# Fixing TensorE's instruction order in a two-layer encoder, and putting weight splits behind the layer norms

## The chip, the cores and the metric

The kernel runs on one core of one Trainium2 chip. The metric is the device time of one execution in microseconds, less is better. The engines named below are TensorE (PE, the matrix products), VectorE (DVE), ScalarE (ACT), GpSimd (POOL) and SyncE (SP, which issues the DMA transfers of the weights).

## The reference

256 tokens of width 1024 and 256 memory tokens go through two layers in float32. Each layer has three residual parts, each followed by a layer norm:

```python
x = layer_norm(x, emb_ln_g, emb_ln_b)
for l in range(2):
    h = hybrid_mixer(x, ...)                     # one product with w_in, then three branches
    x = layer_norm(alpha * x + h, ln_g[l, 0], ln_b[l, 0])
    h = memory_cross_attention(x, mem, ...)      # 4 heads of 256 over the memory's keys and values
    x = layer_norm(alpha * x + h, ln_g[l, 1], ln_b[l, 1])
    h = conv_ffn(x, ...)                         # (silu(conv(gate)) * up) @ w_out, inner width 2816
    x = layer_norm(alpha * x + h, ln_g[l, 2], ln_b[l, 2])
```

The mixer's branches are a differential attention (4 heads, two softmaxes each, rotary positions), a neighbourhood attention (8 heads, a bias for each pair of positions) and a gated short convolution; their results are weighted by gates, summed and multiplied by `w_mix_out`.

## The kernel before

**Products.** Every product is made three times, of operands split into a high and a low part (`mm3`, L243 to L247): high by high (L245), and the two mixed ones (L246, L247). A split (`split_from`, L249 to L251) is two instructions: ACT copies the source, rounded, to the high part (L250), and DVE subtracts that from the source to get the low part (L251). Weights are split so on the chip, and so is every activation that a product reads.

**Weights.** They come as 356 units of 128 x 1024 float32 (512 KB), each used once. `prefetch` (L1090) issues a unit's DMA on SP's queue into one of 4 raw buffers (L1094) and splits it into one of 8 pairs of high and low buffers. It runs 7 units (`LOOK`) ahead of the step that reads the unit. A unit is 24 products of 256 columns, or as many columns in wider products. The first units are the four of the memory's values (`v`) and then those of its keys (`k`); `start` (L480) calls `prefetch(4)` and then `inputs(6)` (L1108), which issues the token tiles, units up to the sixth, and the gain and offset of the first norm (`ln_consts`, DMAs on L1102).

**The order of the work.** The program is a list of steps, made before anything is issued by a planner (`interleave`, L114). Each `Step` has a function, a cost in TensorE time, a latency after which its successor may start, the units it reads and the PSUM banks it takes and gives back. A main sequence is interleaved with side sequences that are spawned (norms, the heads of an attention) and with fills (the products for the memory's keys and values). A unit counts 2.62, the scores of the differential attention have a latency of 5.5, those of the other two attentions 4.0, transposes 1.4 or 1.8. `emit` (L1144) then walks the list, prefetches and calls each step's function.

The list is the program's order. It isn't yet the order in which an engine executes: a scheduler of the compiler orders each engine's instructions by when it reckons them ready, and by priority, which follows the program's order. Only SP is held to the program's order (`manual_schedule`, L1155). PE, ACT and DVE are ordered by the scheduler.

**Places of the list that matter below** (the functions' names; a unit between them in brackets):

- start: the embedding's two norms, then four units of memory values, two units of memory keys, the first transposes of the normed tokens
- layer 1 and alike layer 2, differential attention (`rope` L546 with `swap` L548 and `turn` L554; `diff_group` L568, its score products on L531 and L532): ... `turn`, [vb 3], [gc 0], scores, scores, [gc 1], [gc 2], transposes, transposes, ...
- neighbourhood attention (`near_pair`, L674): [g2 0], scores, scores, [g2 1], [g2 2], transposes, transposes, scores, ...
- cross-attention (`cross_head`, L823): ..., transposes of head 3, scores of head 4, values of head 3, transposes of head 4, values of head 4, a wait for all heads, then the units of the output product (`tok_out`, L872)
- the norm ahead of layer 2's feed-forward: the last products of `tok_out` for token tile 1, two groups of transposes of token tile 0 with the warm-up product (`keep_warm`, L999) between, then the units `fm` of `up_first` (L1005), then `ffn_in` (L1013) and `ffn_out` (L1051)

**The norms.** The residual sum and its statistics (`ln_part`, L345: sum L350, statistics L355) run on DVE as each group of columns is finished. `ln` (L360) then gives a norm step for each of two token tiles (aggregate L368, square root on ACT L369, subtract and scale by the gain L373, reciprocal L385, scale by the deviation and add the offset L378), and transposes on PE (L414), whose results are split (L250, L251) to be the next products' operand. `residual` (L985) spawns the norms of token tiles 0 and 1 after their last products. In the kernel before, `urgent` (L253) records by engine the last norm operation (the sums, statistics, root, scale, and the split of a turned tile), and `behind` (L258) makes the split of each unit prefetched later wait in its engine's order behind the one recorded. The wait is one of order alone. The warm-up product is 8 products of the identity matrix, written to a bank that nothing reads.

Of the kernel before, what the change touches and what calls it, by code (L numbers as in the profile page):

```python
# [21 lines left out]
AF = mybir.ActivationFunctionType  # L22
ALU = mybir.AluOpType
AX = mybir.AxisListType

P = 128
# [168 lines left out]
def rd(t):  # L195
    return t.bitcast(F32)


class Encoder:
    LOOK = 7  # L200
    ACC, ATT = 3, 5
    TB = 10
    BIG = 22
# [45 lines left out]
    def split_from(self, src, ah, al):  # L249
        return (self.nc.scalar.copy(ah, src),  # L250
                self.nc.vector.tensor_tensor(out=al, in0=src, in1=rd(ah), op=ALU.subtract))  # L251

    def urgent(self, ins):  # L253

        self.ahead[ins.ins.engine] = ins.ins.name
        return ins

    def behind(self, ins):  # L258
        name = self.ahead.get(ins.ins.engine)
        if name is not None:  # L260
            self.tc.add_manual_dep(ins.ins, name, NOSYNC, reason="behind a layer norm")

    def proj_f8(self, u, xa, o):

# [71 lines left out]
        return self.tok(n, l, 0, xn, evac, tiles)  # L336


    def ln_consts(self, g, b):
        nc = self.nc  # L340
        self.lng, self.lnb = self.big(), self.big()
        self.load(self.lng, g.partition_broadcast(P))
        self.load(self.lnb, b.partition_broadcast(P))

    def ln_part(self, i, c, acc=None):  # L345

        nc, x = self.nc, self.x[i]
        sl = slice(*c)
        if acc is not None:
            self.urgent(nc.vector.scalar_tensor_tensor(out=x[:, sl], in0=x[:, sl], scalar=ALPHA, in1=acc,  # L350
                                                       op0=ALU.mult, op1=ALU.add))
        if c[0] == 0:
            self.T["st", i] = self.small(24).rearrange("p (c s) -> p c s", c=4)
        for q in range(c[0] // 256, c[1] // 256):
            self.urgent(nc.vector.bn_stats(self.T["st", i][:, q], x[:, 256 * q:256 * q + 256]))  # L355
        if i == 0 and c[0] == 0:

            nc.scalar.activation(self.small(1), self.T["st", 0][:, 0, 0:1], AF.Sqrt, bias=self.epsb, scale=0.0)

    def ln(self, i, nxt, rel, pre=2.6):  # L360

        st = {}
        w = 512 if i == 0 else 256

        def norm():
            nc, x = self.nc, self.x[i]
            mv, rs = self.small(2), self.small(1)
            nc.vector.bn_aggr(mv, self.T["st", i])  # L368
            self.urgent(nc.scalar.activation(rs, mv[:, 1:2], AF.Sqrt, bias=self.epsb, scale=1.0))  # L369

            def sub(h):
                sl = slice(w * h, w * h + w)
                return nc.vector.scalar_tensor_tensor(out=x[:, sl], in0=x[:, sl], scalar=mv[:, 0:1],  # L373
                                                      in1=self.lng[:, sl], op0=ALU.subtract, op1=ALU.mult)

            def scale(h):
                sl = slice(w * h, w * h + w)
                return nc.vector.scalar_tensor_tensor(out=x[:, sl], in0=x[:, sl], scalar=rs,  # L378
                                                      in1=self.lnb[:, sl], op0=ALU.mult, op1=ALU.add)

            if nxt is not None:
                for h in range(D // w):
                    sub(h)
                    if h == 0:
                        nc.vector.reciprocal(rs, rs)  # L385
                    self.urgent(scale(h))
                return

            n, nb = D // w, self.small(1)
            sub(0)  # L390
            nc.vector.reciprocal(rs, rs)
            r = nc.vector.scalar_tensor_tensor(out=nb, in0=mv[:, 0:1], scalar=-1.0, in1=rs,
                                               op0=ALU.mult, op1=ALU.mult)
            sl = slice(w * (n - 1), D)
            nc.scalar.activation(x[:, sl], x[:, sl], AF.Identity, bias=nb, scale=rs)
            nc.gpsimd.tensor_tensor(out=x[:, sl], in0=x[:, sl], in1=self.lng[:, sl], op=ALU.mult)
            nc.gpsimd.tensor_tensor(out=x[:, sl], in0=x[:, sl], in1=self.lnb[:, sl], op=ALU.add)
            for h in range(n - 1):
                if h:
                    self.tc.add_manual_dep(sub(h).ins, r.ins.name, NOSYNC, reason="order of the last rows")  # L400
                scale(h)
            for h in range(n):
                sl = slice(w * h, w * h + w)
                eng = nc.scalar if h % 2 else nc.sync
                eng.dma_start(self.out[i * P:(i + 1) * P, sl], x[:, sl])

        def transp(h):
            nc, n = self.nc, w // P
            if i == 0 and h == 0:
                self.T[nxt] = self.act_tile()  # L410
            a = self.T[nxt]
            pt = self.att()[:, :w].rearrange("p (k t) -> p k t", k=n)
            for k in range(n):
                nc.tensor.transpose(pt[:, k], self.x[i][:, (n * h + k) * P:(n * h + k + 1) * P], self.ident)  # L414
            t, k = n * h // 4, n * h % 4
            for ins in self.split_from(pt, a.his[t][:, k:k + n, i * P:(i + 1) * P],
                                       a.los[t][:, k:k + n, i * P:(i + 1) * P]):
                self.urgent(ins)

        yield Step(norm, 0, pre, rel=rel)  # L420
        if nxt is not None:
            for h in range(D // w):
                yield Step(lambda h=h: transp(h), 0.11 * w / P, 0.3 if h < D // w - 1 else 1.0, acq=1, rel=1)
# [56 lines left out]
    def start(self):  # L480

        nc = self.nc
        self.epsb = self.cst.tile([P, 1], F32, tag="epsb", name="epsb")
        nc.vector.memset(self.epsb, EPS)
        nc.scalar.activation(self.small(1), self.epsb, AF.Sqrt, bias=self.epsb, scale=1.0)
        hi = self.wp.tile([P, 1024], F32R, tag="hi", name=self.nm("hi"), bufs=self.WB)
        lo = self.wp.tile([P, 1024], F32R, tag="lo", name=self.nm("lo"), bufs=self.WB)

        def unit(j, m):
            if j:  # L490
                self.prefetch(j + 1)
                return
            raw, sl = self.t512(), slice(2 * m, 2 * m + 512)
            nc.sync.dma_start(raw, self.aps["w"][0][:, sl])
            self.split_from(raw, hi[:, sl], lo[:, sl])
            if m:
                self.split.append((hi, lo))
        self.load_mem(unit)
        self.prefetch(4)
        self.inputs(6)  # L500
# [406 lines left out]
    def main(self):  # L907
# [7 lines left out]
        for l in range(DEPTH):  # L915
# [55 lines left out]

            um = l == DEPTH - 1
            if um:
                yield Step(self.keep_warm, acq=1, rel=1)
                yield from self.up_first(l, xn, [f"a{l}0", f"a{l}1"])
            yield Wait(f"a{l}0", f"a{l}1")
            yield from self.ffn_in(l, xn, 4 if um else 0)
# [7 lines left out]
    def residual(self, steps, name, xn):  # L985
# [13 lines left out]
    def keep_warm(self):  # L999

        o = self.att()
        for _ in range(8):
            self.nc.tensor.matmul(o[:, :P], self.ident, self.ident, start=True, stop=True)  # L1003

    def up_first(self, l, xn, waits):  # L1005

# [83 lines left out]
    def prefetch(self, upto):  # L1090
        nc = self.nc
        while len(self.split) < min(upto, len(self.order)):
            raw = self.raw()
            nc.sync.dma_start(raw, self.aps["w"][len(self.split)])  # L1094
            hi = self.wp.tile([P, 1024], F32R, tag="hi", name=self.nm("hi"), bufs=self.WB)
            lo = self.wp.tile([P, 1024], F32R, tag="lo", name=self.nm("lo"), bufs=self.WB)
            for ins in self.split_from(raw, hi, lo):
                self.behind(ins)
            self.split.append((hi, lo))

    def load(self, t, src):
# [42 lines left out]
    def emit(ctx, self, tc, aps, out):  # L1144
        nc, PS = tc.nc, bass.MemoryType.PSUM
        self.nc, self.tc, self.aps, self.out = nc, tc, aps, out
        self.uid, self.split, self.bias, self.ahead = 0, [], {}, {}
# [4 lines left out]
        self.sm = ctx.enter_context(tc.tile_pool(name="sm", bufs=4))  # L1152
        self.psa = ctx.enter_context(tc.tile_pool(name="psa", bufs=self.ACC, space=PS))
        self.psb = ctx.enter_context(tc.tile_pool(name="psb", bufs=self.ATT, space=PS))
        with tc.manual_schedule(engines={mybir.EngineType.SP}):  # L1155
            pos = 0
            for s in self.steps:
                if s.units:
                    pos += len(s.units)
                    self.prefetch(pos + self.LOOK)  # L1160
                s.fn(*self.split[pos - len(s.units):pos])


def _layout(a, order):
# [56 lines left out]
```

## Time and profile before

| | before |
|---|---|
| median of 3 executions | 1135.65 us (1134.47 to 1135.90) |
| profiled execution | 1135.06 us |
| its span | 1133.3 us |
| mean granted TensorE clock | 0.994 |
| DMA moved in the span | 208.53 MB, mean 184 GB/s |

The span is the time from the first to the last instruction in the trace; the profiled execution's own time is 1.8 us longer. The clock is the share of full speed that the chip grants TensorE. Rows of the timeline give the start, the duration of all instructions of the row together (overlaps counted once), engine, line, operation, output <- inputs, and the number of instructions; in brackets stands the engine's idle time before the row and what ended it. Products are pipelined: a duration of 0.28 us for one doesn't mean that the next starts 0.28 us later. The 356 units are most of the DMA traffic, and a unit's transfer lands a median of 4.0 us after its issue.

### The profile page before, as it was taken

The page shows a single profiled execution, that of the slowest core. Times are in us where ns is not written, and L with a number is a line of the kernel's source. Part 1 is how long each engine was busy: PE and PEld are TensorE (multiplying, and loading weights), DVE is VectorE, ACT ScalarE, POOL GpSimd, SP SyncE. Part 2 cuts the span into 40 slices and gives each one's busy share as a digit, 9 for nine tenths or more (in the row PEclk, how much of TensorE's full clock was granted, in tenths as well). Part 3 has the DMA queues.
Part 4 walks back from the last instruction along what each step waited for, and adds up shares of the span by engine and source line. Part 5 has one row for each costly group of instructions (what it writes and reads, how often), then busy time and mean ns, then how long its engine had stood idle before and what let it go on. Part 6 is the DMA issues. An engine that isn't in the chain of part 4 may idle for free.

```text
span 1133.3 us, 18595 instructions
## 1 busy us (share of the span) xinstructions
PE 1103.8 (97%) x7340; PEld 1014.8 (90%) x7340; DVE 798.9 (70%) x1198; ACT 612.7 (54%) x958; POOL 12.4 (1%) x18
## 2 busy tenths in 40 slices
PE   7999999999999999999999999999999979999997
PEld 6899998888898999998889999888889879999986
DVE  6788888666864876665586888865787576666644
ACT  5556767445453565554445667744536436555540
POOL 0000000000000000000000000000000000000001
PEclk9999999999999999999999999999999989999999
DMA  8785437567563666565747544556746444665551
GB/s 297 245 262 170 136 135 232 183 189 241 168 186 99 200 204 186 182 181 189 263 143 231 174 148 167 179 185 197 256 145 201 140 149 150 186 185 180 182 180 37
DMA packets 60471, 208.53 MB, mean 184 GB/s; under 512 B 7008, under 2 KB 8288, under 8 KB 60384
## 3 DMA queue, kind: packets, MB, share of 16 engines
q1 hardware_dynamic: 59952, 206.83, 56.9%
q8 instruction: 57, 0.93, 0.3%
q10 hardware_dynamic: 432, 0.52, 0.1%
q14 instruction: 30, 0.25, 0.1%
HBM read 204.18 MB, written 1.05 MB: 181 GB/s over the span
## 4 chain that ended last, share of the span: by engine, by line
PE 66%; DVE 3%; ACT 1%; DMA 1%; issue 1%; DVEq 0%; ACTq 0%; SPq 0%
PE acc L245 18%; PE acc L246 18%; PE acc L247 18%; PE att L246 3%; PE att L247 3%; PE att L245 3%; DMA raw<-in_w_dram 1%; DVE lo L251 1%; PE att L414 0%; ACT hi L250 0%; DVE s L355 0%; DVE big L251 0%; PE att L617 0%; PE att L851 0%; PE att L1003 0%
## 5 line engine op out<-in xcount | busy, mean ns | idle before, releaser
L251 DVE TENSOR_TENSOR lo<-raw,hi 128x1024 fp32r<-128x1024 f32 x355 | 431.8, 1222 | 237.1 <-ACT hi L250 235.6
L250 ACT CAST hi<-raw 128x1024 fp32r<-128x1024 f32 x355 | 370.7, 1050 | 333.1 <-PE acc L246 155.5
L245 PE MATMUL acc<-big,hi 128*128 128x256 f32 x1376 | 391.0, 285 | 3.1 <-ACT big L294 1.2
L246 PE MATMUL acc<-big,hi 128*128 128x256 f32 x1376 | 390.2, 284 | 1.9 <-DVE big L251 1.9
L247 PE MATMUL acc<-big,lo 128*128 128x256 f32 x1376 | 390.2, 284 | 0.6 <-DVE lo L251 0.6
L245 PEld LDWEIGHTS acc<-big,hi 128*128 128x128 f32 x1376 | 263.3, 192 | 5.1 <-ACT big L294 1.8
L246 PEld LDWEIGHTS acc<-big,hi 128*128 128x128 f32 x1376 | 263.6, 192 | 3.0 <-DVE big L251 2.6
L247 PEld LDWEIGHTS acc<-big,lo 128*128 128x128 f32 x1376 | 263.6, 192 | 1.2 <-DVE lo L251 1.1
L245 PE MATMUL acc<-hi,big 128*128 128x512 f32 x584 | 230.1, 396 | 6.1 <-ACT hi L250 6.0
L246 PE MATMUL acc<-lo,big 128*128 128x512 f32 x584 | 230.8, 395 | 0.5 <-DVE lo L251 0.5
L247 PE MATMUL acc<-hi,big 128*128 128x512 f32 x584 | 228.0, 393 | 0.0
L245 PEld LDWEIGHTS acc<-hi,big 128*128 128x128 f32 x584 | 110.5, 190 | 27.1 <-ACT hi L250 6.5
L247 PEld LDWEIGHTS acc<-hi,big 128*128 128x128 f32 x584 | 110.7, 190 | 23.0
L246 PEld LDWEIGHTS acc<-lo,big 128*128 128x128 f32 x584 | 110.9, 190 | 21.2 <-DVE lo L251 1.2
L246 PE MATMUL att<-lo,big 128*128 128x256 f32 (+1 forms) x228 | 72.6, 319 | 0.0
L245 PE MATMUL att<-hi,big 128*128 128x256 f32 (+1 forms) x228 | 72.4, 318 | 0.0
L247 PE MATMUL att<-hi,big 128*128 128x256 f32 (+1 forms) x228 | 72.3, 318 | 0.0
L250 ACT CAST big<-att 128x512 fp32r<-128x512 f32 (+2 forms) x64 | 28.1, 458 | 45.8 <-PE att L247 25.8
L251 DVE TENSOR_TENSOR big<-att,big 128x512 fp32r<-128x512 f32 (+2 forms) x64 | 32.1, 518 | 27.7 <-ACT big L250 27.2
L245 PEld LDWEIGHTS att<-hi,big 128*128 128x128 f32 x228 | 43.3, 190 | 4.9
L246 PEld LDWEIGHTS att<-lo,big 128*128 128x128 f32 x228 | 43.3, 190 | 4.5
L247 PEld LDWEIGHTS att<-hi,big 128*128 128x128 f32 x228 | 43.3, 190 | 3.1
(145 smaller groups left out, 948.2 us busy)
## 6 DMA issues: line engine op xcount, KB each, us to landing
raw<-in_w_dram SPq DMA_DIRECT2D x355, 512.0 KB, 4.0
t<-in_bias_dram SPq DMA_DIRECT2D x16, 256.0 KB, 5.5
big<-in_ln_g_dram SPq DMA_DIRECT2D x6, 512.0 KB, 5.5
big<-in_ln_b_dram SPq DMA_DIRECT2D x6, 512.0 KB, 6.2
raw<-in_memT_dram SPq DMA_DIRECT2D x6, 512.0 KB, 4.4
big<-big SPq DMA_DIRECT2D x16, 128.0 KB, 2.3
x<-in_x_dram SPq DMA_DIRECT2D x4, 256.0 KB, 7.9
t<-in_memT_dram SPq DMA_DIRECT2D x3, 256.0 KB, 7.9
```

Of the source, the lines that this page charges most:

```text
L245: mm(o, lh, rh, start=first, stop=False)
L246: mm(o, lh, rl, start=False, stop=False)
L247: mm(o, ll, rh, start=False, stop=last)
L250: return (self.nc.scalar.copy(ah, src), self.nc.vector.tensor_tensor(out=al, in0=src, in1=rd(ah), op=ALU.subtract))
L251: self.nc.vector.tensor_tensor(out=al, in0=src, in1=rd(ah), op=ALU.subtract))
```

## The change

TensorE is held to the program's order, as SP is. The instructions of a norm (sums and statistics, the norm step, the transposes and splits of the turned tile) are traced with a priority as if they stood 2000 instructions earlier. A list `parts` keeps the two split instructions of every unit. `hold` records the last four norm operations of an engine (the root on ACT, the last scale on DVE, the splits of a turned tile on both) and puts the splits of all units from position `pos + 4` on behind them, those already traced too; `behind` does the same for units prefetched later. The sums and statistics are recorded no more. The warm-up step and its function are removed.

```diff
 class Encoder:
     LOOK = 7
+    NEAR = 4
...
-    def urgent(self, ins):
-
-        self.ahead[ins.ins.engine] = ins.ins.name
-        return ins
-
-    def behind(self, ins):
-        name = self.ahead.get(ins.ins.engine)
-        if name is not None:
-            self.tc.add_manual_dep(ins.ins, name, NOSYNC, reason="behind a layer norm")
...
+    def ahead(self):
+
+        return self.tc.high_priority(offset=2000)
+
+    def hold(self, ins):
+
+        names = self.last.setdefault(ins.ins.engine, [])
+        names.append(ins.ins.name)
+        del names[:-4]
+        for parts in self.parts[self.pos + self.NEAR:]:
+            self.behind(parts)
+
+    def behind(self, parts):
+        for p in parts:
+            for name in self.last.get(p.ins.engine, ()):
+                self.tc.add_manual_dep(p.ins, name, NOSYNC, reason="behind a layer norm")
+
...
     def ln_part(self, i, c, acc=None):
 
+        with self.ahead():
+            self.ln_sum(i, c, acc)
+
+    def ln_sum(self, i, c, acc):
...
         def norm():
+            with self.ahead():
+                normalise()
+
+        def normalise():
...
-                    self.urgent(scale(h))
+                    done = scale(h)
+                self.hold(root)
+                self.hold(done)
                 return
...
         def transp(h):
+            with self.ahead():
+                turn(h)
+
+        def turn(h):
...
-                self.urgent(ins)
+                self.hold(ins)
...
             if um:
-                yield Step(self.keep_warm, acq=1, rel=1)
                 yield from self.up_first(l, xn, [f"a{l}0", f"a{l}1"])
...
-            for ins in self.split_from(raw, hi, lo):
-                self.behind(ins)
+            self.parts.append(self.split_from(raw, hi, lo))
+            self.behind(self.parts[-1])
             self.split.append((hi, lo))
...
-        with tc.manual_schedule(engines={mybir.EngineType.SP}):
-            pos = 0
+        with tc.manual_schedule(engines={mybir.EngineType.SP, mybir.EngineType.PE}):
             for s in self.steps:
                 if s.units:
-                    pos += len(s.units)
-                    self.prefetch(pos + self.LOOK)
-                s.fn(*self.split[pos - len(s.units):pos])
+                    self.pos += len(s.units)
+                    self.prefetch(self.pos + self.LOOK)
+                s.fn(*self.split[self.pos - len(s.units):self.pos])
```

More of the change, by code (lines that the diff above doesn't have):

```diff
@@ L349, in ln_part @@
         if acc is not None:
-            self.urgent(nc.vector.scalar_tensor_tensor(out=x[:, sl], in0=x[:, sl], scalar=ALPHA, in1=acc,
-                                                       op0=ALU.mult, op1=ALU.add))
+            nc.vector.scalar_tensor_tensor(out=x[:, sl], in0=x[:, sl], scalar=ALPHA, in1=acc,
+                                           op0=ALU.mult, op1=ALU.add)
         if c[0] == 0:
@@ L354, in ln_part @@
         for q in range(c[0] // 256, c[1] // 256):
-            self.urgent(nc.vector.bn_stats(self.T["st", i][:, q], x[:, 256 * q:256 * q + 256]))
+            nc.vector.bn_stats(self.T["st", i][:, q], x[:, 256 * q:256 * q + 256])
         if i == 0 and c[0] == 0:
@@ L368, in norm @@
             nc.vector.bn_aggr(mv, self.T["st", i])
-            self.urgent(nc.scalar.activation(rs, mv[:, 1:2], AF.Sqrt, bias=self.epsb, scale=1.0))
+            root = nc.scalar.activation(rs, mv[:, 1:2], AF.Sqrt, bias=self.epsb, scale=1.0)
             def sub(h):
@@ L494, in unit @@
             nc.sync.dma_start(raw, self.aps["w"][0][:, sl])
-            self.split_from(raw, hi[:, sl], lo[:, sl])
+            parts = self.split_from(raw, hi[:, sl], lo[:, sl])
             if m:
+                self.parts.append(parts)
                 self.split.append((hi, lo))
@@ L997, in residual @@
         yield Spawn(f"{name}1", self.ln(1, xn, 2 if name[0] != "f" else 3, 3.4))
[L999 to L1003, printed above, removed]
     def up_first(self, l, xn, waits):
@@ L1146, in emit @@
         self.nc, self.tc, self.aps, self.out = nc, tc, aps, out
-        self.uid, self.split, self.bias, self.ahead = 0, [], {}, {}
+        self.uid, self.split, self.bias = 0, [], {}
+        self.pos, self.parts, self.last = 0, [], {}
         self.cst = ctx.enter_context(tc.tile_pool(name="cst", bufs=1))
```

## Prediction

> **What bounds the kernel now.** I read the page's head first: if TensorE (PE) is the bound, only the microseconds in which it stands or runs slowly can be won or lost.
>
> ```profile
> span 1133.3 us, 18595 instructions
> PE 1103.8 (97%) x7340; PEld 1014.8 (90%) x7340; DVE 798.9 (70%) x1198; ACT 612.7 (54%) x958; POOL 12.4 (1%) x18
> ```
>
> PE is busy 1103.8 of 1133.3 us, VectorE (DVE) 70%, ScalarE (ACT) 54%. So 29.5 us is all that better ordering could ever save, while every wait put into PE's stream adds its full length. The view of busy time by stretches gives PE's pace in an undisturbed stage and its speed in a disturbed one (columns: length, then PE, weight loads, DVE, ACT and POOL busy, granted clock, DMA share, GB/s).
>
> ```profile
> 400.00:420.00 20.00, 20.00 (x169) 20.00 (x169) 15.83 (x26) 13.61 (x21) 0.00 (x0) 1.00 0.71 214
> 927.80:934.60 6.80, 4.10 (x20) 4.13 (x21) 6.80 (x17) 0.88 (x2) 0.00 (x0) 0.50 0.45 151
> ```
>
> 169 products in 20.00 us are 0.118 us each, so a unit of weights (24 products) takes 2.84 us. In that stretch no wait is left: the order of the queues already hides DVE and ACT there. The view of PE's waits says where they aren't hidden (total, times, longest):
>
> ```profile
> PE att L414 <- DVE x L378: 6.6, 2, 6.2
> PE acc L245 <- ACT hi L250: 6.0, 2, 4.6
> PE acc L246 <- DVE big L251: 1.9, 3, 1.3
> PE acc L245 <- ACT big L294: 1.2, 1, 1.2
> PE att L532 <- DVE big L521: 0.9, 1, 0.9
> ```
>
> One large wait, for a norm (L378); the rest is small. The scores (L532) wait for the rope once, the attention's values not at all in the first lines. Whether that is because the Vector work is quick, or because the scheduler put other products there, decides the case.
>
> **The change, part by part.** All terms are against the profiled execution: 1135.06 us, its span of 1133.3 and 1.8 around it. The median shown, 1135.65, is 0.6 higher, and I add that at the end.
>
> **A, the norm in layer 2 and the warm-up product.** On PE:
>
> ```profile
> 930.50 1.09 PE L414 MATMUL att<-ident,x 128*128 128x128 f32 x4 [6.20 <-DVE x L378]
> 931.38 3.50 PE L1003 MATMUL att<-ident 128*128 128x128 f32 x16
> 934.72 0.60 PE L414 MATMUL att<-ident,x 128*128 128x128 f32 x4
> ```
>
> and what DVE did meanwhile:
>
> ```profile
> 920.83 1.21 DVE L251 TENSOR_TENSOR lo<-raw,hi 128x1024 fp32r<-128x1024 f32 x1
> 921.95 1.01 DVE L350 SCALAR_TENSOR_TENSOR x<-x,att 128x512 f32<-128x512 f32 x2
> ...
> 925.00 0.25 DVE L368 BATCH_NORM_AGGREGATE s<-s 128x2 f32<-128x24 f32 x1
> 925.16 0.36 DVE L350 SCALAR_TENSOR_TENSOR x<-x,att 128x256 f32<-128x256 f32 x1
> 925.44 2.35 DVE L251 TENSOR_TENSOR lo<-raw,hi 128x1024 fp32r<-128x1024 f32 x2
> 927.71 1.41 DVE L373 SCALAR_TENSOR_TENSOR x<-x,s,big 128x512 f32<-128x512 f32 x2
> ...
> 929.67 1.34 DVE L378 SCALAR_TENSOR_TENSOR x<-x,s,big 128x512 f32<-128x512 f32 x2
> ```
>
> PE ran out at 930.50 − 6.20 = 924.30 and turned the last part of row tile 0 at 934.72: 10.4 us, of which only the first four transposes are work (0.3 at full clock, half of the 0.60 row). Lost: 10.1. The cause is weight splits (L251, 1.2 each) inside the norm: one at 920.83 ahead of the residual sum, two at 925.44 ahead of L373; and the warm-up product, whose 3.50 us run at a clock of 0.50, in front of the second transposes. With the norm's operations first, a norm that three splits delay no more has its aggregate (925.00) some 3 us earlier, near 922; then L373 and L378 for the first half (half of 1.41 and of 1.34) with the other tile's sums between end by about 924.3, the second half by 925.8. What is late next is the split of the turned tile, 0.59 on ACT and 0.69 on DVE (rows in F), 1.3 us with nothing in the list between. So 10.1 − 1.3 = −8.8. The waits for L246 <- DVE big L251 (1.9), also the turned tile's or a norm's split, and the other 0.4 of L414 I count as gone: A = **−11.1**, between −12.0 and −8.
>
> The row of 927.80 shows what the removed step could act on, the clock: after 3.5 us without products PE gets 0.50 for some 7 us. With A's wait cut to 1.3 nothing needs warming here.
>
> **B, the first norm and the memory's keys.** Units 0 to 3 are memory values, 4 and 5 memory keys; both keys are traced before the embedding's two norms, at position 0, so `hold` puts their splits, as units from 4 on, behind the norms' last operations. Those need the gain vector's DMA, issued as the first row shows (start, then us to issue; below it, us to landing):
>
> ```profile
> 13.38 0.33 SPq L1102 DMA_DIRECT2D big<-in_emb_ln_g_dram  x1
> ```
> ```profile
> big<-in_emb_ln_g_dram SPq DMA_DIRECT2D x1, 512.0 KB, 7.6
> ```
> ```profile
> 24.16 2.99 DVE L373 SCALAR_TENSOR_TENSOR x<-x,s,big 128x512 f32<-128x512 f32 x6
> 27.07 0.68 DVE L251 TENSOR_TENSOR big<-acc,big 128x512 fp32r<-128x512 f32 x1
> 27.68 2.98 DVE L378 SCALAR_TENSOR_TENSOR x<-x,s,big 128x512 f32<-128x512 f32 x6
> ```
> ```profile
> 22.25 0.28 PE L247 MATMUL acc<-big,lo 128*128 128x256 f32 x1
> ```
>
> It lands at 13.38 + 7.6 = 20.98; the norms' 2.99 + 2.98 and 0.2 of small ones end at 27.1; then the split of k0, 1.2 (as at 920.83), is ready at 28.4. PE, which takes k0's third product at 22.25 and may no longer take anything else, waits 6.1 us. Behind it on PE stands everything; DVE and ACT go on. A wait of that length is followed by the slow clock of the row of 927.80: 6.80 us at 0.50 with 4.10 busy, so half of 4.10 is lost, 2.0. B = 6.1 + 2.0, **+8.1**; at least 5 (PE later by 1 us at 22), at most 9 (the 0.68 of L251 between).
>
> [...]
>
> **C, rope and scores, in each layer.** Now PE may not reorder. Before:
>
> ```profile
> 87.86 0.99 PE L531 MATMUL att<-big,big 128*128 128x256 f32 x4
> 89.80 0.35 PE L532 MATMUL att<-big,big 128*128 128x256 f32 x1 [0.94 <-DVE big L521]
> ```
> ```profile
> 88.44 2.46 DVE L521 TENSOR_TENSOR big<-big,big 64x1024 fp32r<-64x1024 f32 x2
> ```
>
> In the planner's list the first scores stand behind one conv unit (gc 0), but the scheduler put a second one in front of them. In the list's order they come one unit earlier, 87.86 − 2.84 = 85.0, while the low half of the turned keys is done at 88.44 + 2.46 = 90.9. L531 runs first (four of them some 0.5), so the wait is up to 5.4 us; if the two splits' worth of DVE time that stood before L521 goes behind it, 3.0. I take the middle, 4.2, less the 0.94 there now: +3.3, twice, **+6.6**.
>
> **D, softmax of the differential attention, E, of the near one.** The last product of a pair's scores, and the end of the Vector chain that the next transposes need:
>
> ```profile
> 94.22 0.28 PE L532 MATMUL att<-big,big 128*128 128x256 f32 x1
> ```
> ```profile
> 104.92 0.88 DVE L598 SCALAR_TENSOR_TENSOR t<-t,s,t 128x256 f32<-128x256 f32 x2
> ```
> ```profile
> 157.31 0.28 PE L532 MATMUL att<-big,big 128*128 128x256 f32 x1
> ```
> ```profile
> 165.41 0.62 DVE L697 TENSOR_SCALAR t<-t,s 128x256 f32<-128x256 f32 x2
> ```
>
> D: 105.80 − 94.50 = 11.3 us. In the list two units and the first pair's transposes lie between, 2 × 2.84 + 0.5 = 6.2: 5.1 short. Weight splits share that chain, and a PE that waits frees no weight buffers, so splits stop and the chain gets shorter: I take half, +2.5, twice, **+5.0** (0 to 10). E: 166.03 − 157.6 = 8.4 against two units and 0.4, 6.1: 2.3 short, half is 1.2, twice, **+2.4** (0 to 12, should all four head pairs wait).
>
> **F, the end of cross-attention.** There the list holds, after head 4's scores, only the values of head 3, then transposes, then values; the units of the output product come after a wait for all heads. Before, PE filled this with those units.
>
> ```profile
> 898.78 0.69 DVE L835 TENSOR_REDUCE s<-att 128x2 f32<-128x512 f32 x1
> ...
> 901.02 0.62 DVE L843 TENSOR_SCALAR t<-t,s 128x256 f32<-128x256 f32 x2
> ...
> 906.10 0.69 DVE L251 TENSOR_TENSOR t<-att,t 128x512 fp32r<-128x512 f32 x1 [0.21 <-ACT t L250]
> ```
> ```profile
> 905.48 0.59 ACT L250 CAST t<-att 128x512 fp32r<-128x512 f32 x1 [0.32 <-PE att L851]
> ```
>
> Softmax: 901.64 − 898.78 = 2.9 us, against 12 products of head 3's values, 1.4: a wait of 1.5. Then the split of the turned weights, 905.48 to 906.79, 1.3, with no cover. 2.85 in all, twice, **+5.7** (to 9).
>
> The splits that wait behind norms cost nothing where four units (11.4 us of products) lie in hand. Sum: −11.1 + 8.1 + 6.6 + 5.0 + 2.4 + 5.7 = +16.7, 1151.8 profiled. With 0.6: 1152.4, given as 1152.
>
> **Rivals.** A difference of 0.2%, 2.3 us, is about what a measurement of this kernel can tell from none.
>
> *Faster, the queues re-form.* DVE's order is made anew around a fixed PE: if what the scores and values need is put first, C, D and E vanish. Then A −11.1, the waits for big L294 and L521 −2.1, B at its low end +5 and F +5.7: −2.5, so 1133 in the median; with B gone as well (third rival) 1128. For it: DVE is idle 30% of the time and ACT 46%, and the chains hold splits that could wait. Against: in the present trace the scheduler, free to choose, moved units in front of the scores. It decides if C, D and E come to nothing together, or, with B gone, stay under 5 us. Chance 0.25.
>
> *Held splits come too late.* Behind each of the five later pairs of norms two splits (2.4) stand between the last norm operation and PE's next unit, if four units are not in hand. 5 × 2.4 = +12: 1164. Against it: the norms' 2.99 + 2.98 and some 4 of sums and turned splits, an estimate from the rows in A, are under 11.4. Chance 0.12.
>
> *The holds on splits already traced have no effect* (the split of k0 needs nothing from the norm and may be fixed ahead of it): B is gone, 1144, still slower. Chance 0.10.
>
> *Nothing to measure:* gains and losses cancel, 1135. Chance 0.07.
>
> **How the numbers follow.** The forecast has 0.46. Slower is that with 0.12 and 0.10: 0.68; same 0.07; faster 0.25. The likeliest case alone runs from 1138 (D and E at nothing, C at its low 3.0, B 5, A −12.0: +2.8) to 1167 (D and E at their upper ends, the others as taken: +31.3). The range takes most of the faster rival in: 1131 to 1168.
>
> **What would show it.** Right: PE waits for DVE lo L251 some 6 us near 22 us, and a clock near 0.50 behind it; waits of L532 <- DVE big L521 of 3 to 5 us near 88 and once more in layer 2; waits of the cross-attention's transposes for L843 (about 1.5) and of its values for t L251 (about 1.3); L414 <- DVE x L378 down from 6.2 to under 1.5, and no L1003. Wrong: no wait near 22 us (B), waits of the three attentions under 1 us each (C, D, E), or a new PE wait for lo L251 in the units behind each norm.

## The result, and the profile after

| | before | after |
|---|---|---|
| median | 1135.11 us (4 executions) | 1177.62 us (4, 1174.19 to 1179.28) |
| ratio | | 1.0379 (95%: 1.0361 to 1.0398) |
| profiled execution, its span | 1135.06, 1133.3 us | 1177.24, 1175.5 us |
| mean granted TensorE clock | 0.994 | 0.984 |

The change makes the kernel 42 us slower. 1152 was forecast, with 1168 as the upper end: the sign was right, the size was not. The head of the page after:

```profile
span 1175.5 us, 18578 instructions
...
PE 1117.3 (95%) x7324; PEld 1020.4 (87%) x7324; DVE 800.5 (68%) x1198; ACT 615.0 (52%) x958; POOL 12.4 (1%) x18
```

PE does 16 passes less (the warm-up product), and is yet busy 13.5 us longer, most of it by a slow clock (worked out below, under the prediction). The rest of the 42.2 us, 28.7, is time without a product. DVE and ACT are busy nearly as long as before (800.5 us against 798.9, 615.0 against 612.7). The waits of PE (total, times, longest; the new kernel's L246 to L248 are the old L245 to L247, L251/L252 the two halves of a split, L554/L555 the scores):

```profile
PE att L728 <- DVE t L720: 7.5, 5, 1.9
PE acc L248 <- DVE lo L252: 7.0, 1, 7.0
PE acc L246 <- ACT hi L251: 5.2, 2, 4.6
PE att L554 <- ACT big L539: 4.0, 2, 2.0
PE att L874 <- DVE t L866: 3.7, 3, 1.7
PE att L247 <- DVE t L252: 3.5, 6, 1.2
PE att L555 <- DVE big L544: 3.5, 4, 1.2
PE att L629 <- DVE t L621: 3.3, 2, 2.1
...
PE att L436 <- DVE x L394: 0.2, 1, 0.2
```

Where one long wait for a norm stood (L414, now L436: 6.6, now 0.2) there are now some forty short ones, at softmaxes, turned tiles' splits and ropes, and one of 7.0 at the start. No line is above 7.5; all lines together come to 49.7 us, against 20.7 before.

Where the time came from, stage by stage: the end of the last product of the same unit in both traces, at places where all earlier work of the list is done in both.

| up to the end of | before | after | loss of the stage | forecast |
|---|---|---|---|---|
| second unit of `qa`, layer 1 (start) | 54.1 | 59.9 | +5.8 | +8.1 |
| `kb`, layer 1 (rope, differential attention) | 151.8 | 164.3 | +6.7 | +5.8 |
| gates `g1`, layer 1 (neighbourhood attention) | 259.9 | 282.7 | +10.3 | +1.2 |
| `mo`, layer 1 (merging, output) | 291.2 | 316.0 | +2.0 | 0 |
| `xo`, layer 1 (norm, cross-attention) | 373.7 | 405.7 | +7.2 | +2.85 |
| third unit of `ka`, layer 2 (norms, feed-forward) | 614.6 | 645.4 | −1.2 | with the norms −2.3 |
| `kb`, layer 2 | 697.9 | 736.0 | +7.3 | +5.8 |
| first unit of `w0`, layer 2 (neighbourhood attention) | 759.0 | 804.7 | +7.5 | +1.2 |
| `mo`, layer 2 | 837.5 | 884.9 | +1.8 | 0 |
| `xo`, layer 2 | 924.3 | 975.4 | +3.7 | +2.85 |
| last unit of `ffn_out` (norm, feed-forward) | 1116.7 | 1158.9 | −8.9 | −8.8 |

The losses sum to 42.2. The last row is as forecast, rope and differential attention nearly (6.7 and 7.3 for 5.8); the neighbourhood attention's two rows are far off (10.3 and 7.5 for 1.2). That stage on PE in the changed kernel, layer 1:

```profile
176.35 0.81 PE L728 MATMUL att<-ident,t 128*128 128x128 f32 x4 [1.92 <-DVE t L720]
178.50 1.08 PE L728 MATMUL att<-ident,t 128*128 128x128 f32 x4 [1.34 <-DVE t L720]
187.53 0.51 PE L246 MATMUL acc<-hi,big 128*128 128x512 f32 x1 [0.98 <-ACT t L797]
190.81 0.38 PE L246 MATMUL att<-t,big 128*128 128x256 f32 x1 [0.91 <-ACT t L251]
192.19 0.39 PE L247 MATMUL att<-t,big 128*128 128x256 f32 x1 [0.99 <-DVE t L252]
...
205.55 0.72 PE L728 MATMUL att<-ident,t 128*128 128x128 f32 x4 [1.35 <-DVE t L720]
```

Two waits for softmax results (the first and the second pair of heads), then one for a gate's activation, then two for the splits of turned weights, and one more for the softmax of a later pair; each is the work of another engine behind a PE that may take nothing else.

The norm in layer 2, the one place that gains, on DVE and then on PE:

```profile
971.22 0.26 DVE L384 BATCH_NORM_AGGREGATE s<-s 128x2 f32<-128x24 f32 x1
971.52 1.42 DVE L389 SCALAR_TENSOR_TENSOR x<-x,s,big 128x512 f32<-128x512 f32 x2
972.85 0.16 DVE L401 RECIPROCAL s<-s 128x1 f32<-128x1 f32 x1
972.92 0.40 DVE L362 SCALAR_TENSOR_TENSOR x<-x,att 128x256 f32<-128x256 f32 x1
973.24 1.41 DVE L394 SCALAR_TENSOR_TENSOR x<-x,s,big 128x512 f32<-128x512 f32 x2
```
```profile
975.26 1.03 PE L436 MATMUL att<-ident,x 128*128 128x128 f32 x8
...
976.54 0.50 PE L246 MATMUL acc<-hi,big 128*128 128x512 f32 x1 [0.24 <-ACT big L251]
```

No weight split stands between the norm's operations any more; their results are there at 974.65 (973.24 + 1.41), before the last products of token tile 1, and all eight transposes follow without a wait.

### The profile page after: what moved, and what is told of

Its sections match the earlier page's. It is cut to its first block, busy times and chain, and to the rows that moved or that the text cites. A ratio compares the mean times of both kernels' runs of the same rounds, so it can differ in the third digit from the quotient of the medians.

```text
span 1175.5 us, 18578 instructions
## 1 busy us (share of the span) xinstructions
PE 1117.3 (95%) x7324; PEld 1020.4 (87%) x7324; DVE 800.5 (68%) x1198; ACT 615.0 (52%) x958; POOL 12.4 (1%) x18
## 3 DMA queue, kind: packets, MB, share of 16 engines
HBM read 204.18 MB, written 1.05 MB: 175 GB/s over the span
## 4 chain that ended last, share of the span: by engine, by line
PE 82%; DVE 7%; ACT 5%; issue 3%; DMA 3%; SPq 0%; DVEq 0%; ACTq 0%
PE acc L246 23%; PE acc L247 22%; PE acc L248 22%; PE att L247 4%; PE att L248 4%; PE att L246 4%; DVE lo L252 1%; ACT hi L251 1%; ACT t L613 1%; DVE big L252 1%; DMA raw<-in_memT_dram 1%; PE att L436 1%; DMA t<-in_memT_dram 1%; PE att L640 1%; DMA big<-in_emb_ln_g_dram 1%
## 5 line engine op out<-in xcount | busy, mean ns | idle before, releaser
L252 DVE TENSOR_TENSOR lo<-raw,hi 128x1024 fp32r<-128x1024 f32 x355 | 432.8, 1223 | 268.9 <-ACT hi L251 264.2
L251 ACT CAST hi<-raw 128x1024 fp32r<-128x1024 f32 x355 | 371.6, 1050 | 370.7 <-PE acc L247 145.4
L248 PE MATMUL acc<-big,lo 128*128 128x256 f32 x1376 | 390.7, 284 | 7.0 <-DVE lo L252 7.0
L246 PE MATMUL acc<-big,hi 128*128 128x256 f32 x1376 | 393.3, 286 | 1.0 <-ACT hi L251 0.6
L247 PE MATMUL acc<-big,hi 128*128 128x256 f32 x1376 | 390.8, 284 | 0.7 <-DVE big L252 0.7
L248 PEld LDWEIGHTS acc<-big,lo 128*128 128x128 f32 x1376 | 265.3, 193 | 7.2 <-DVE lo L252 7.2
L246 PEld LDWEIGHTS acc<-big,hi 128*128 128x128 f32 x1376 | 265.6, 193 | 1.8 <-ACT hi L251 1.1
L247 PEld LDWEIGHTS acc<-big,hi 128*128 128x128 f32 x1376 | 265.4, 193 | 1.2 <-DVE big L252 0.9
L246 PE MATMUL acc<-hi,big 128*128 128x512 f32 x584 | 233.2, 399 | 7.2 <-ACT hi L251 4.6
L247 PE MATMUL acc<-lo,big 128*128 128x512 f32 x584 | 230.2, 394 | 0.6 <-DVE lo L252 0.6
L248 PE MATMUL acc<-hi,big 128*128 128x512 f32 x584 | 229.1, 392 | 0.0
L246 PEld LDWEIGHTS acc<-hi,big 128*128 128x128 f32 x584 | 111.0, 190 | 29.9 <-ACT hi L251 5.4
L248 PEld LDWEIGHTS acc<-hi,big 128*128 128x128 f32 x584 | 110.6, 189 | 24.3 <-DVE big L252 0.4
L247 PEld LDWEIGHTS acc<-lo,big 128*128 128x128 f32 x584 | 110.9, 190 | 22.1 <-DVE lo L252 2.4
L248 PE MATMUL att<-hi,big 128*128 128x256 f32 (+1 forms) x228 | 72.6, 318 | 0.0
L247 PE MATMUL att<-lo,big 128*128 128x256 f32 (+1 forms) x228 | 72.6, 318 | 0.0
L246 PE MATMUL att<-hi,big 128*128 128x256 f32 (+1 forms) x228 | 72.4, 317 | 0.0
L251 ACT CAST big<-att 128x512 fp32r<-128x512 f32 (+2 forms) x64 | 28.5, 453 | 41.7 <-PE att L436 32.6
L246 PEld LDWEIGHTS att<-hi,big 128*128 128x128 f32 x228 | 43.3, 190 | 4.8
L247 PEld LDWEIGHTS att<-lo,big 128*128 128x128 f32 x228 | 43.3, 190 | 4.6
L248 PEld LDWEIGHTS att<-hi,big 128*128 128x128 f32 x228 | 43.3, 190 | 3.0
L252 DVE TENSOR_TENSOR big<-att,big 128x512 fp32r<-128x512 f32 (+2 forms) x64 | 32.7, 517 | 15.1 <-ACT big L251 13.0
```

Source lines behind the costliest of these rows:

```text
L246: mm(o, lh, rh, start=first, stop=False)
L247: mm(o, lh, rl, start=False, stop=False)
L248: mm(o, ll, rh, start=False, stop=last)
L251: return (self.nc.scalar.copy(ah, src), self.nc.vector.tensor_tensor(out=al, in0=src, in1=rd(ah), op=ALU.subtract))
```

## The experiments

Medians come with the ratio to the kernel before on the same chip. Line numbers differ by a few between these kernels: L728 and L730 are the same transposes, L720 and L722 the same scaling.

**TensorE's order alone, and everything but it.**

```diff
-        with tc.manual_schedule(engines={mybir.EngineType.SP}):
+        with tc.manual_schedule(engines={mybir.EngineType.SP, mybir.EngineType.PE}):
```

> The kernel before with one edit: TensorE is held to the program's order; norms, holds and the warm-up product stay as before. Theory P (the order alone costs the time, in the attentions): 1135 + 42 (all) + 12 (the norm's gain absent) - 6 (the hold at the start absent) = about 1183, with the waits for L531/L532, the softmax results and turned splits that the changed kernel shows. Theory H (holds and priorities put the attentions' Vector and Scalar work late, and the order matters little): within 10 us of before, 1135 to 1145.

Measured 1183.64 us, ratio 1.0440 (1.0422 to 1.0458). As theory P has it: the one line makes the whole loss and a little more.

The reverse edit in the changed kernel (SP alone held):

> The changed kernel with one edit: TensorE is again ordered by the scheduler. Theory P: the attentions' waits go, the norm's gain of about 12 stays, the start costs at most the 6 it does now: 1124 to 1131, faster than before. Theory H: the waits in the attentions stay, 1165 to 1180.

Measured 1134.59, ratio 1.0009 (1.0000 to 1.0018). The attentions' waits are gone, so theory H falls; but no gain is left. The start is 4.2 us later than in the kernel before (58.3 against 54.1 in the table's first row), and two rows of PE show where the gain of the last norm went:

```profile
925.96 1.84 PE L436 MATMUL att<-ident,x 128*128 128x128 f32 x8 [3.16 <-DVE x L394]
```
```profile
953.54 0.58 PE L246 MATMUL acc<-big,hi 128*128 128x256 f32 x1 [3.44 <-DVE fa L1061]
```

The norm's wait is half of what it was, and PE leaves the norm 6.4 us ahead of the kernel before (1.5 of it from earlier stages). Then 4.5 of it is given back by 953.54: with the order free, the first gates of the feed-forward are begun among the units of `fm`, and a later one waits until DVE has read the accumulator that it needs (`fa`).

**The warm-up product put back.**

```diff
+                yield Step(self.keep_warm, acq=1, rel=1)
                 yield from self.up_first(l, xn, [f"a{l}0", f"a{l}1"])
```

> The changed kernel with the warm-up product back in its place. Both theories: with only a wait of about 0.2 left at that norm the clock is up, so the product costs its own 16 passes, 1 to 3.5 us: 1178 to 1181. If the removal were what costs time elsewhere (the clock of the first feed-forward units), 1170 or less.

Measured 1178.39, ratio 1.0404 (1.0386 to 1.0422), against 1.0379 (1.0361 to 1.0398) without it: no difference that these runs can tell. Removing it costs nothing here.

**The hold at the start.**

```diff
     def hold(self, ins):
 
+        if self.pos == 0:
+            return
```

> The changed kernel, holds left out while the list stands at its first step, so that the memory keys' splits need not wait for the embedding's norms. If the wait of 7.0 us near 22 us is that hold: it goes, with some slow clock behind it, 1169 to 1172. If the keys' split waits for Vector work in any case (the norms have the higher priority): 1175 to 1178.

Measured 1169.28, ratio 1.0323 (1.0307 to 1.0339), so the hold costs 6 (by the ratios) to 8 us (by the medians) of the 42; the wait of 7.0 that ended at 28.6 us goes, and one of 2.0 comes that ends at 29.4 us. Without the hold and with TensorE free:

> Norm operations ahead and holds, TensorE free, no warm-up product, no hold at the first step. Its twin with that hold was 4.2 us behind the kernel before when the first layer's products began: without it 1129 to 1132. If that start loss comes from the norms' priority instead of the hold: 1134 to 1135.

Measured 1129.05, ratio 0.9962 (0.9949 to 0.9975): 5 below its twin with the hold. Both pairs agree with step B.

**A gain kept.** TensorE free up to the second cross-attention's output, held from there:

```diff
+        cut = next(n for n, s in enumerate(self.steps) if ("xo", 1, 0) in s.units)
+        for engines, steps in (({sp}, self.steps[:cut]), ({sp, pe}, self.steps[cut:])):
+            with tc.manual_schedule(engines=engines):
```

> As the run before, but TensorE held to the program's order from the first output unit of the second cross-attention to the end, and free ahead of it. In the changed kernel that stretch was 11.7 us shorter than before; with TensorE free it gained 4.9 at the norm and gave 4.5 back in a wait for the feed-forward's gate (fa). If holding the order is what keeps that gain: 1121 to 1125. If the gain hangs on what comes ahead (full buffers, splits in hand): 1129 to 1133.

Measured 1121.43, ratio 0.9895 (0.9882 to 0.9908). This is the fastest of all the kernels here. Its waits:

```profile
PE acc L246 <- ACT hi L251: 6.9, 2, 4.6
PE acc L246 <- ACT big L285: 2.4, 2, 1.2
PE acc L246 <- ACT big L251: 1.2, 3, 0.7
```

The first is the start's loads; nothing else is above 2.4. Held in the same stretch, with the old handling of the norms and without the warm-up product:

> The kernel before, its old handling of the norms, without the warm-up product, TensorE held only from the first output unit of the second cross-attention on. If the order alone makes the gain at layer 2's feed-forward: 1125 to 1128 (the run with only TensorE's order changed gained 6 there). If it needs the norms' raised priority too: 1130 to 1133.

Measured 1130.70, ratio 0.9974 (0.9964 to 0.9984). So the held end with the old norms gains 0.3%, the norms' priority with the order free 0.4%, and both together 1.05%, more than the sum of the two. Priority alone loses its gain at the last norm again at the gates, and the held order alone still has splits inside the norm.

**Why the waits in the attentions are that long: planned latencies.** All kernels from here on are without the hold at the start, so 1169.28 is what they start from.

```diff
-        yield Step(scores, 0.87, 4.0, acq=2, rel=2)
+        yield Step(scores, 0.87, 8.5, acq=2, rel=2)
```

> The changed kernel, no hold at the first step (1169.3 that way), and one number of the planner changed: latency of the neighbourhood attention's scores 8.5 instead of 4.0, the time that its softmax took in the changed kernel. If the loss comes from a list planned with too short a latency: the 10.3 + 6.2 us lost in the two layers' neighbourhood attentions go, 1152 to 1156. If holding TensorE costs whatever the list says, the waits move elsewhere: 1164 to 1172.

Measured 1171.52, ratio 1.0331 (1.0313 to 1.0349). The waits for softmax results went from the first row to the second:

```profile
PE att L730 <- DVE t L722: 7.8, 5, 1.9
```
```profile
PE att L730 <- DVE t L722: 6.9, 2, 3.5
```

Fewer and longer. The second pair's results now came 13 us after its scores. Then the other latencies as well:

> As the run with the near attention's latency, and the other attentions' latencies as measured too: differential scores 8 (was 5.5), cross-attention scores 6 (was 4), turned softmax 2.0 and 2.4 (was 1.4 and 1.8), rope 9.5 (was 6). Latency theory: most of the 14 us of rope and differential attention and of the 13 us of cross-attention go as well, 1126 to 1138. Rival (holding costs in any list): above 1155.

Measured 1174.26, ratio 1.0374 (1.0355 to 1.0393). The longer latency alone (the first of these two runs) refutes the latency theory for the neighbourhood attention. The second run settles less, as one part of it was badly made: the rope's number is a delay ahead of its own Vector work, so the larger one moved the rope later (the waits for L545 became 8.0).

**Priority.** The same raised priority for rope, scores, softmax and transposes:

```diff
-        yield Step(scores, 0.87, 4.0, acq=2, rel=2)
+        yield Step(self.first(scores), 0.87, 4.0, acq=2, rel=2)
...
```

> The changed kernel, no hold at the first step (1169.3 that way), the list as it is, and the instructions of rope, scores, softmax and its transposes traced with the same raised priority as the norms. Queue theory (the waits come from Vector and Scalar queues that put weight splits and other pairs' work between a softmax's own operations): 1140 to 1153. Rival, duration theory (a softmax takes that long by itself and the list gives it too little time): above 1163.

Measured 1170.09, ratio 1.0322 (1.0308 to 1.0337): nothing. With both:

> The raised priority of the run before together with the longer planned latencies. Queue theory with latency as the second part: below the run before by 5 to 15, 1130 to 1145. If longer latencies only let more splits come between, as the two runs with latencies alone suggest: no better than the run before.

Measured 1176.66, ratio 1.0379 (1.0363 to 1.0395): worse than with priority alone. The rope is late in this run too, so it shows only that these latencies and priority together don't help.

**The weight splits taken out of the softmax's way**, by a shorter prefetch and by holds.

```diff
-    LOOK = 7
+    LOOK = 6
```

> The changed kernel, no hold at the first step (1169.3 that way), weights prefetched 6 units ahead instead of 7, so that a split's target buffer was freed one unit (2.8 us) earlier. Theory S (on Scalar's and Vector's queues a softmax stands behind a weight split that waits until TensorE has finished the unit whose buffer it takes): the waits for softmax results shrink by 1 to 2.8 each, 1150 to 1160. If the queues' own work is what takes long: 1167 to 1175.

Measured 1169.59, ratio 1.0322 (1.0305 to 1.0339).

> Weights prefetched 5 units ahead. Theory S: the target buffers are free long before, waits at the softmaxes as with 6 or less; 1145 to 1160, unless transfers come too late (waits for hi L251 <- DMA). Without theory S: 1170 or more, from later transfers.

Measured 1168.24, ratio 1.0306 (1.0288 to 1.0324).

```diff
+            self.hold(ex)
+            self.hold(sc)
             st["e"] = bias
```

> The changed kernel, no hold at the first step, and the splits of units four and more ahead held behind the last exponential and the last scaling of each softmax, as the change does for norms. Theory S: softmax results come 2 to 3 us earlier, 1145 to 1158, unless the held splits come too late for the units behind them (new waits for lo L252 or hi L251). If a softmax's own operations take that long: no gain at the softmax waits, 1167 or more.

Measured 1171.63, ratio 1.0341 (1.0326 to 1.0357). All three intervals overlap that of the run that they start from (1.0307 to 1.0339). Yet the softmax waits did shrink, from 7.8 us to these (prefetch of 6, of 5, held splits):

```profile
PE att L730 <- DVE t L722: 4.8, 5, 1.6
```
```profile
PE att L730 <- DVE t L722: 3.4, 3, 1.4
```
```profile
PE att L734 <- DVE t L724: 1.8, 2, 0.9
```

So theory S was right that splits stood in the softmax's way, and wrong about what that is worth: other waits grew instead, with the held splits above all those for the turned weights (2.9 us in the run they start from):

```profile
PE att L246 <- ACT t L251: 9.1, 4, 2.4
```

What is left without splits is shown by the run with a prefetch of 5, from the first scaling of scores to the result that PE's second transposes take at 173.00 (columns: length, then PE, weight loads, DVE, ACT, POOL busy, clock, DMA):

```profile
164.70:173.10 8.40, 7.42 (x41) 6.20 (x40) 7.93 (x23) 6.32 (x19) 0.00 (x0) 1.00 0.01 2
```
```profile
164.71 1.29 DVE L713 SCALAR_TENSOR_TENSOR t<-att,t 128x512 f32<-128x512 f32 x2 [0.28 <-PE att L557]
...
166.51 0.68 DVE L713 SCALAR_TENSOR_TENSOR t<-att,t 128x512 f32<-128x512 f32 x1
...
170.73 0.68 DVE L715 TENSOR_REDUCE s<-t 128x2 f32<-128x512 f32 x1
...
171.98 1.14 DVE L722 TENSOR_SCALAR t<-t,s 128x256 f32<-128x256 f32 x4
```

DVE is busy 7.93 of 8.40 us and does not split one unit; nearly all of it is two softmaxes, interleaved, about 4 us each. The list starts all four pairs together, and gives each a latency as if DVE were its own. That this is the cause is an argument so far; the next run tests it.

**Pairs apart.** So the remedy would not be a longer latency, but to space them:

```diff
-        yield Step(scores, 0.87, 4.0, acq=2, rel=2)
+        yield Step(scores, 0.87, 7, acq=2, rel=2)
...
-                yield Spawn(f"na{l}{t}", self.near_pair(l, t), 1.0)
+                yield Spawn(f"na{l}{t}", self.near_pair(l, t), 1.0 + 11 * t)
```

> The changed kernel, no hold at the first step (1169.3 that way), and in the planner's list the neighbourhood attention's four pairs of heads started 11 apart instead of all at once, each with a latency of 7. Theory V (two pairs scored back to back share VectorE: each needs over 4 us of its own there, so the second one's results come after 8 us and more whatever else is in the queue): the two layers' near waits of 12 us and the slow clock behind them go, 1152 to 1158. If holding costs in any list, as the longer latencies alone suggested: 1166 to 1172.

Measured 1152.98, ratio 1.0171 (1.0150 to 1.0193): 16 us less, as theory V has it. Two numbers were changed at once, but a latency of 8.5 without the spacing had gained nothing. The line of L730 is gone from the waits, and the stage is full:

```profile
160.00:210.00 50.00, 49.62 (x263) 41.70 (x262) 42.54 (x81) 32.32 (x66) 0.00 (x0) 1.00 0.50 170
```

Cut at the places of the table above, the two neighbourhood stages no longer lose anything against the kernel before (0.0 and −1.1 us, where the changed kernel lost 10.3 and 7.5).

> As the run before, and the differential attention's four groups 8 apart, the first one 3 later (one unit more for the rope), latency 7. Theory V: of the 14 us lost in the two layers' ropes and differential attentions most go, 1140 to 1146. Rival: no better than the run before.

Measured 1149.68, ratio 1.0140 (1.0112 to 1.0169), short of what was expected: rope and differential attention still lose 6.7 and 5.7 us in the two layers. The scores' waits fell (L554 and L555 had 7.5 in the changed kernel), but the last group now ends later, and the transposes of the attention's output wait for it:

```profile
PE att L642 <- ACT t L633: 7.1, 4, 3.4
...
PE att L557 <- DVE big L546: 2.8, 4, 0.8
```

## Why the prediction was right or wrong

**A was right.** The stage lost −8.9 where −8.8 was worked out; the norm's wait is 0.2 and the warm-up product costs nothing to remove. The agreement is closer than the working: the split of the turned tile, taken at 1.3, shows as a wait of 0.24, and the other norms gave 1.2 where 2.3 was taken. That the gain needs the held order (the free one gives 4.5 back) I had not seen.

**B was right in its mechanism.** The wait is 7.0 against 6.1, for the named operation:

```profile
28.61 0.58 PE L248 MATMUL acc<-big,lo 128*128 128x256 f32 x1 [6.97 <-DVE lo L252]
```
```profile
20.92 3.00 DVE L389 SCALAR_TENSOR_TENSOR x<-x,s,big 128x512 f32<-128x512 f32 x6 [0.29 <-DMA big<-in_emb_ln_g_dram]
23.84 0.68 DVE L252 TENSOR_TENSOR big<-acc,big 128x512 fp32r<-128x512 f32 x1
24.44 2.99 DVE L394 SCALAR_TENSOR_TENSOR x<-x,s,big 128x512 f32<-128x512 f32 x6
27.35 4.62 DVE L252 TENSOR_TENSOR lo<-raw,hi 128x1024 fp32r<-128x1024 f32 x4
```

The gain vector, both norms, the 0.68 in between, then the splits: the chain as forecast. The stage lost 5.8, net of start waits that it had before, the hold by itself 6 to 8; 8.1 was forecast. The slow clock came too (0.50 from 24.6 to 31.5 us), but PE has only 2.8 us of work in it, so it costs under 1.5 and not 2.0, and the kernel before has 3.4 us of work at 0.50 near 13 us that the changed one has not. The rival that the hold has no effect on traced splits is refuted by that.

**C and D were about right**, 6.7 and 7.3 a layer for 5.8, in part by luck. The rope's wait is 3.5 (2.0, 1.0 and 0.5 at 93 to 96 us) where 4.2 was taken, and its larger part in layer 1 is for ACT (L539), not for the low half that was named; the differential softmax's (L629) is 1.1 and 2.1 for 2.5. A slow clock behind the rope's waits, for which no term stood, makes up for what is missing.

**E failed: the term of the neighbourhood attention, "half is 1.2, twice, +2.4 (0 to 12)".** It measured +10.3 and +7.5, and is 15 of the 25 us by which the sum was short. Two steps failed. The first is the halving, "splits stop and the chain gets shorter". Splits did not stop, and the chain got longer: from the last score product of two pairs to the third of their four results it is 178.62 − 168.97 = 9.7 us, against the 8.4 read before.

```profile
168.69 0.28 PE L555 MATMUL att<-big,big 128*128 128x256 f32 x1
```
```profile
168.78 1.22 DVE L252 TENSOR_TENSOR lo<-raw,hi 128x1024 fp32r<-128x1024 f32 x1
...
173.21 1.22 DVE L252 TENSOR_TENSOR lo<-raw,hi 128x1024 fp32r<-128x1024 f32 x1
...
178.00 0.62 DVE L720 TENSOR_SCALAR t<-t,s 128x256 f32<-128x256 f32 x2
```

Two pairs at once on DVE do the rest. So the first transposes wait 3.3 us in layer 1 (1.92 and 1.34) and 2.9 in layer 2, where 1.2 was taken. The second step, and the larger, is that the term ends there. Behind the first transposes come 4.6 us of waits in layer 1 and 2.2 in layer 2, for the gate, the turned weights' splits and, in layer 1, a later pair; and in both layers PE works 3.15 and 5.86 us at a clock of 0.50, which costs nearly half of that. None of these had a term; only the upper end, 12, allowed for waits of all four pairs. Starting the pairs apart removes the whole loss of this stage.

**F was right in kind and half in size.** At the tail of layer 1 PE waits 0.97, 0.68 and 0.34 us, 2.0 against 2.85; but the first heads wait too (1.71 and 0.58 at 345 us, with a slow clock behind them), and 2.0 and 1.8 were lost in merging and output, for which no term stood.

**The clock was counted once, at B.** Ahead of the end it is 0.50 in six stretches of the changed kernel (they are listed in the last section) and in two of the kernel before (13.03 to 16.44 and 927.80 to 934.62 us). The sums over these stretches (length, then busy time of each engine):

```profile
sum 34.15, PE 26.26 PEld 24.27 DVE 29.71 ACT 12.77 POOL 1.30; mean PE 4.38 PEld 4.05 DVE 4.95 ACT 2.13 POOL 0.22
```
```profile
sum 10.23, PE 7.53 PEld 6.78 DVE 9.50 ACT 3.52 POOL 0.00; mean PE 3.77 PEld 3.39 DVE 4.75 ACT 1.76 POOL 0.00
```

Products of 256 columns start 0.21 us apart at a clock of 0.50 (at 350 us) and 0.12 at full clock (at 353), so PE loses nearly half of its busy time there: by this estimate 12 to 13 us, against under 4 before. Of the 42.2 us, then, some 9 are the clock, 28.7 are missing cover, and 4 to 5 (of the 13.5 that PE is busy longer) are not accounted for.

The faster rival failed on its own condition: C, D and E did not vanish. Putting the softmax first in the queues, by priority or by holding the splits back, made E no cheaper in the total. "Held splits come too late" isn't seen: no wait for lo L252 or hi L251 behind the later norms is in the list; the two lines that bear these names are waits of the start.

## What to carry to other kernels

A list in program order is a schedule only if it accounts for every engine's capacity, not for a latency of each step alone: two softmaxes that are started together share VectorE (busy 7.93 of the 8.40 us, about 4 us for each, in the run with a prefetch of 5), and the second one's results come as late as the work of both. Before an order is fixed on the bounding engine, list for each of its waits what the free scheduler has put there, and hold the order only in the stretch where it gains (here the last norm, 7.6 us from 1129.05 to 1121.43). If a longer latency and a priority change nothing, look at whose operations fill the queue during the wait, and look at the other waits before calling a theory refuted: a wait that shrinks may come back at the next step (with the held splits the softmax waits fell from 7.8 to 1.8 us, and those for the turned weights rose from 2.9 to 9.1).

## What the runs showed of the hardware that was not expected

The clock fell after shorter waits than the one that the prediction took from the kernel before, where PE was without products for 3.5 us ahead of the fall (924.30 to 927.80). PE of the changed kernel is full up to 343.3 us, then waits 1.71 us for the cross-attention's first transposes, and its clock is 0.50 from 345.5 to 352.3, through a second wait of 0.58 and some 5 us of work. Yet waits of 0.98, 0.91 and 0.99 between 186 and 193 us left it at 1.00.

The six stretches of the changed kernel ahead of the end with a clock of 0.50, and PE's waits at the fall or in the 5 us ahead of it:

| clock 0.50, us | PE's waits (us, and where they end) |
|---|---|
| 24.63 to 31.46 | 0.63 (21.14), 6.97 (28.61; the clock fell 3.0 us into it) |
| 92.89 to 99.71 | 2.01 (92.94) |
| 178.23 to 181.65 | 1.92 (176.35), 1.34 (178.50) |
| 345.48 to 352.30 | 1.71 (345.04) |
| 666.33 to 669.75 | 2.01 (664.03), 1.21 (665.62), 0.78 (666.87) |
| 748.25 to 755.09 | 1.92 (748.02) |

In this trace the length of a single wait does not tell whether a slow stretch follows: one of 1.71 us was followed by 0.50, and one of 2.15 was not. The two waits, then the stretch behind the first and the one that holds the second (columns as above; the clock is the number behind POOL's count):

```profile
345.04 1.03 PE L874 MATMUL att<-ident,t 128*128 128x128 f32 x4 [1.71 <-DVE t L866]
```
```profile
678.27 0.74 PE L629 MATMUL att<-ident,t 128*128 128x128 f32 x4 [2.15 <-DVE t L621]
```
```profile
345.48:352.30 6.82, 6.24 (x28) 5.75 (x28) 4.74 (x8) 2.80 (x7) 0.00 (x0) 0.50 0.49 163
669.75:748.25 78.50, 73.97 (x583) 71.45 (x581) 56.44 (x98) 51.43 (x107) 1.90 (x2) 1.00 0.41 135
```

What decides between them is not shown. The six slow stretches lasted 3.4 to 6.8 us, with 2.85 to 6.24 us of PE's work in each; a wait of about two microseconds cost such a stretch in one place and none in another.
